# A fused Mamba-2 and pooling block: the first stage's weight subtractions move from GpSimd to VectorE, and the chain from dt gets priority

## The chip, the core and the metric

The kernel runs on one core of a Trainium2 chip. TensorE multiplies, VectorE and ScalarE do elementwise work and move results out of PSUM, GpSimd does a few elementwise operations, and SyncE issues the DMAs. Each engine works its own queue strictly in order and waits on semaphores of the others. The metric is the device time of one execution in microseconds (us), as the median of the runs.

## What is computed

One decoder block over 512 tokens of width 1024, all in float32. The first half, which the change touches:

```python
mod = (silu(c) @ w_ada + b_ada)                       # 6 vectors of 1024: shift, scale, gate, twice
h = rmsnorm(x, norm_mix_w) * (1.0 + scale_m) + shift_m
proj = h @ w_in                                       # z 2048, xbc 3072, dt 32, pool 1024, gates 2048
z, xbc, dt_raw, u_pool, gate_logits = split(proj)
xbc = silu(causal_depthwise_conv(xbc, conv_w, conv_b))
dt = softplus(dt_raw + dt_bias)
a_cont = -exp(a_log)
y = ssd_chunked_scan(x32 * dt, dt * a_cont, bmat, cmat)   # 4 groups of 8 heads, 4 chunks of 128 tokens
# in the scan: a_cs = cumsum(dt * a_cont); decay exp(a_cs[l] - a_cs[s]); states carried over the chunks
```

After it come the skip and the gate by silu(z), a group norm, the branch products, the pooling mixer, the merge, and an MLP with squared ReLU.

## The kernel before

Activations lie transposed: 128 channels on the partitions, 512 tokens along the row. Each float32 product is made of three matmuls in a fast format: a weight block is split into a rounded high half (ScalarE casts it, L131) and the remainder (a subtraction, L132), and so is the activation; high by high, high by low and low by high are summed (`mm3`, L141 to L143). A `unit` is eight blocks of 128 by 128 against h, 24 matmuls into one PSUM bank.

**The first stage (L216 to L283)** is written in the order that the engines keep (`manual_schedule`). ScalarE takes the Silu of c (L225) and TensorE spreads it over the partitions; ScalarE copies that to `cbc` (L235). ScalarE squares the eight tiles of x (L232), VectorE adds the squares as a tree (L230), TensorE sums over the partitions (L164), and `rstd` makes R, the reciprocal norm, spread over partitions in a PSUM bank (L176 to L185). `warm(n)` (L211) issues n small matmuls without a use. Then eight steps, k = 0 to 7, each for 128 channels of h:

- `ada(j)` (L157) forms 128 entries of the vector `mod` on VectorE, from a transfer of 512 KB: a product with `cbc`, summed along the row, and a short read of the accumulator. Each step needs two, the scale and the shift of its channels.
- L250 turns a scale into `amod` = (1 + scale) * norm weight; L265 scales x by it and by R; L266 (ScalarE) adds the shift and rounds to the high half; L271 forms the low half.
- the weights for step k (`wstart`, 896 columns: dt padded to 128, then B, C and four tiles of xs for group 0) are loaded, cast on ScalarE and subtracted on **GpSimd** (`load_unit(..., pool)`, L132), two steps ahead; GpSimd also copies dt's 32 low columns next to the high ones (L268), so that two matmuls do for dt what takes three elsewhere.
- TensorE runs 18 matmuls (L281) into six banks and two for dt (L283) into a seventh.

**Behind it** a scheduler orders the instructions by the order of the code and by priority. ScalarE copies the six banks out (L294). Then **the chain from dt** (L299 to L338): bias (L305), four transposes (L308), softplus as a series on VectorE (L311 to L325, with one exponential, L314, on ScalarE), times -exp(a_log) (L315, L326), cumulative sums by a triangular matmul (L328), `ncs` (L329), transposes back (L332), and the sums and their exponentials to DRAM (L333 to L336), from where they come back spread over partitions (`mt`, L424; L484). `conv` (L344 to L350) makes the convolution and Silu of the six tiles.

**A group of the scan** (`ssd_group`, a generator) goes through its four chunks: mt and its exponentials (L424 to L433), transposes of xs (L437), times dt (`xdt`, L439). It yields, and other units are issued in between. After the yield come the state products: `xd`, the decayed inputs (L451), and their matmul (L454), then the rest of the chunk.

Buffers are slots handed out first in, first out: 50 of 512 columns (`S`), four for raw weights (`RAW`), eight for split weights (`HL`), and eight PSUM banks, three of them (`PU`) for units and five (`PS`) for the rest. The order in which code gives a slot back decides who gets it next.

Of the kernel before, what the change touches and what calls it, by code (L numbers as in the profile page):

```python
# [19 lines left out]
NC = 4  # L20
# [12 lines left out]
NPAR = _n  # L33
# [25 lines left out]
def block_kernel(tc, xT, crow, arow, par, adaT, wstart, wz, wx, wpool_in, wgate, wpw, wbs, wbp, wout, wup, wdn, out):  # L59
    nc = tc.nc  # L60
    act, dve, pool, pe, sp = nc.scalar, nc.vector, nc.gpsimd, nc.tensor, nc.sync

    with (
# [12 lines left out]
        S = slots("s", NSLOT)  # L76
# [9 lines left out]
        par_t = sb.tile([P, NPAR + 0], F32, name="par_t")  # L86
# [129 lines left out]
        with tc.manual_schedule():  # L216
            raw0 = RAW.get()
            crow_t = raw0[:1]
            sp.dma_start(crow_t, crow)
            xs0 = [S.get() for _ in range(8)]  # L220
            for k in range(8):
                sp.dma_start(xs0[k], xT[k])
            sp.dma_start(par_t[:, :NPAR], par)
            warm(6)
            act.activation(crow_t, crow_t, AF.Silu)  # L225
            cps = [PU.get(), PU.get()]
            for i in range(2):
                pe.matmul(cps[i], ones[:1, :], crow_t[:, i * T:(i + 1) * T], start=True, stop=True)
            sq = [S.get() for _ in range(8)]
            add = lambda i, j: dve.tensor_tensor(sq[i], sq[i], sq[j], ALU.add)  # L230
            for k in range(8):
                act.activation(sq[k], xs0[k], AF.Square)  # L232
                if k in (4, 6):
                    i = k // 2 - 2
                    act.copy(cbc[:, i * T:(i + 1) * T], cps[i])  # L235
                for i, j in ((), ((0, 1),), (), ((2, 3), (0, 2)), (), ((4, 5), (0, 4)), ((0, 6),), ((0, 7),))[k]:
                    add(i, j)
            ssum = sq[0]
            S.put(*sq[1:])
            PU.put(*cps)  # L240
            RAW.put(raw0)
            warm(10)
            ps = PU.get()
            column_sums(ps, [ssum], 0, NC)
            S.put(ssum)
            warm(4)
# [6 lines left out]
            scale(0)  # L253
            R = rstd(ps, DM, 0, NC, S)
            PU.put(ps)
            warm(8)
            ada(0, EARLY)
            first = [PS.get() for _ in range(8 - NPU)] + [PU.get() for _ in range(NPU - 1)]
            ws = [load_unit(wstart[i], 896, pool) for i in range(2)]
            for k in range(8):  # L260
                hi, lo = S.get(F32R), S.get(F32R)
                h.append((hi, lo))
                t = S.get()
                shift = mod[:, k:k + 1]
                dve.scalar_tensor_tensor(t, xs0[k], amod[:, k:k + 1], R, ALU.mult, ALU.mult)  # L265
                act.activation(hi, t, AF.Identity, bias=shift)  # L266
                w = ws.pop(0)
                pool.tensor_copy(w[0][0][:, NH:2 * NH], w[0][1][:, :NH].bitcast(F32))  # L268
                if 0 < k < 7:
                    scale(k + 1)  # L270
                dve.scalar_tensor_tensor(lo, t, shift, hi.bitcast(F32), ALU.add, ALU.subtract)  # L271
                S.put(t)
                if k == 0:
                    scale(1)
                if k < 7:
                    ada(k + 1, EARLY)
                if k < 6:
                    ws.append(load_unit(wstart[k + 2], 896, pool))
# [8 lines left out]
        SZ.put(*early[2:])  # L287

        took = [None]
        for u in range(1, 7):  # L290
# [3 lines left out]
            act.copy(took[u], first[u])  # L294
        PU.put(*first[8 - NPU:])
        PS.put(*first[1:8 - NPU])


        r_ = slice(0, NH)  # L299
        w_ = NC * NH  # L300
        v, cs_t, ecs_t = S.get(), S.get(), S.get()
        tmp = [S.get() for _ in range(4)]
        sp.dma_start(ea, arow[0:1, :].broadcast_to([P, NH]))
        e, s, s2, q = (t[:, :w_] for t in tmp)
        act.activation(v[:2 * NH], first[0][:2 * NH], AF.Identity, bias=col("dtb", rows=2 * NH))  # L305
        tk = PU.get()
        for c in range(NC):
            pe.transpose(tk[:, 2 * c * NH:2 * (c + 1) * NH], v[:2 * NH, c * P:(c + 1) * P], ident[:2 * NH, :2 * NH])  # L308
        dtf, ncf = dtk.rearrange("p c h -> p (c h)"), ncs.rearrange("p c h -> p (c h)")
        both = tk[:, :2 * w_].rearrange("p (c a h) -> p c a h", c=NC, a=2)  # L310
        dve.tensor_copy(dtk, both[:, :, 0, :])  # L311
        dve.tensor_tensor(dtk, dtk, both[:, :, 1, :], ALU.add)
        dve.scalar_tensor_tensor(e, dtf, -1.0, dtf, ALU.mult, ALU.max)
        act.activation(e, e, AF.Exp, scale=-1.0)  # L314
        act.activation(ea, ea, AF.Exp)  # L315
        dve.tensor_scalar(s, e, 2.0, None, ALU.add)
        dve.reciprocal(s, s)
        dve.tensor_tensor(s, s, e, ALU.mult)
        dve.tensor_tensor(s2, s, s, ALU.mult)
        dve.tensor_scalar(q, s2, 1.0 / 15, None, ALU.mult)  # L320
        for d in (13, 11, 9, 7, 5, 3):
            dve.scalar_tensor_tensor(q, q, 1.0 / d, s2, ALU.add, ALU.mult)
        dve.scalar_tensor_tensor(q, q, 1.0, s, ALU.add, ALU.mult)
        dve.tensor_scalar(dtf, dtf, 0.0, None, ALU.max)
        dve.scalar_tensor_tensor(dtf, q, 2.0, dtf, ALU.mult, ALU.add)  # L325
        dve.tensor_tensor(  # L326
            q.rearrange("p (c h) -> p c h", c=NC), dtk, ea.unsqueeze(1).broadcast_to([P, NC, NH]), ALU.mult)
        pe.matmul(tk[:, :w_], tri, q, start=True, stop=True)  # L328
        dve.tensor_copy(ncf, tk[:, :w_])  # L329
        tk2 = first[0]  # L330
        for c in range(NC):
            pe.transpose(tk2[r_, c * P:(c + 1) * P], ncs[:, c, :], ident)  # L332
        act.activation(cs_t[r_], tk2[r_], AF.Copy, scale=-1.0)  # L333
        act.activation(ecs_t[r_], tk2[r_], AF.Exp, scale=-1.0)
        sp.dma_start(cs_d, cs_t[r_])
        sp.dma_start(ecs_d, ecs_t[r_])  # L336
        PU.put(tk)
        S.put(v, cs_t, ecs_t, *tmp)  # L338


        def conv(ps, j, o=None):
# [61 lines left out]
        def ssd_group(g):  # L403
# [17 lines left out]
            for c in range(NC):  # L421
# [14 lines left out]
                for i in range(4):  # L436
# [2 lines left out]
                dve.tensor_tensor(  # L439
                    v3(xdt), v3(ps), dtk[:, c, heads].unsqueeze(2).broadcast_to([P, HG, 64]), ALU.mult)  # L440
                PS.put(ps)
                yield
                yo = None
                if c > 0:
# [2 lines left out]
                        pe.matmul(yo[:, i * P:(i + 1) * P], prev[:, i * P:(i + 1) * P], cT[:, cc],  # L447
                                  start=True, stop=True)
                if c < 3:
                    xd = S.get()  # L450
                    dve.tensor_tensor(  # L451
                        v3(xd), v3(xdt), decg[:, c, :].unsqueeze(2).broadcast_to([P, HG, 64]), ALU.mult)
# [12 lines left out]
                    prev = nprev  # L465
# [367 lines left out]
```

## Time and profile before

| | us |
|---|---|
| median of 3 runs (lowest, highest) | 998.27 (997.61, 998.98) |
| the profiled execution | 997.95 |
| its span, first to last instruction | 996.2 |
| TensorE busy in the span | 973.7 (98%) |
| VectorE busy | 623.8 (63%) |
| ScalarE busy | 482.3 (48%) |
| GpSimd busy | 84.7 (9%) |

Times in the profile count from the start of the span. The busy time of TensorE is modelled from pipelined matmuls: a matmul of 512 columns shows a duration of some 390 ns, and the next one starts 0.23 us after it began. So the distance of two starts, not the duration, is what a matmul costs in a full stretch. In an idle time the releaser named is the one that came last.

### The profile page before, as it was taken

Reading aid. Unit: us, or ns where it says so; the run is one execution under the profiler, and the core shown is the slowest. Engines: PE = TensorE matmul, PEld = TensorE weight load, DVE = VectorE, ACT = ScalarE, POOL = GpSimd, SP = SyncE. Lnnn points to the kernel's source line nnn. Section 1 sums busy time; section 2 is a strip of 40 time slices with the busy share of each in tenths; the row PEclk is TensorE's granted clock in tenths of the full one; section 3 lists DMA queues with packets and bytes.
Section 4 is the critical chain, followed back from the end, with each engine's and each line's share of the span. In section 5 each row is a group of like instructions: output and inputs, shape, how many; then the busy total and the mean of one; then the engine's idle time right before and its main releaser. Section 6 shows DMA issues by size and latency. Waiting matters only on the chain.

```text
span 996.2 us, 12196 instructions
## 1 busy us (share of the span) xinstructions
PE 973.7 (98%) x4732; PEld 802.8 (81%) x4732; DVE 623.8 (63%) x887; ACT 482.3 (48%) x718; POOL 84.7 (9%) x79
## 2 busy tenths in 40 slices
PE   7899999999999999999999999999999999999996
PEld 6678777888778878788888888988888888888886
DVE  5978877586777776979775565654344334434443
ACT  5277999579648932553422343443133223313342
POOL 3510210211012012210000000000000000000000
PEclk8999999999999999999999999999999999999998
DMA  9725542442354233436886444032323232232302
GB/s 355 278 92 172 152 124 91 125 136 88 90 134 125 88 114 95 127 106 220 279 272 200 137 167 162 1 111 101 101 89 106 85 106 89 102 106 85 106 1 85
DMA packets 58620, 129.55 MB, mean 130 GB/s; under 512 B 4609, under 2 KB 29313, under 8 KB 58562
## 3 DMA queue, kind: packets, MB, share of 16 engines
q1 hardware_dynamic: 58562, 128.77, 40.1%
q8 instruction: 37, 0.61, 0.3%
q14 instruction: 21, 0.17, 0.1%
HBM read 126.53 MB, written 2.23 MB: 129 GB/s over the span
## 4 chain that ended last, share of the span: by engine, by line
PE 79%; ACT 8%; DVE 7%; DMA 2%; issue 2%; POOL 1%; SPq 1%; DVEq 0%; ACTq 0%; POOLq 0%
PE ps L141 25%; PE ps L142 24%; PE ps L143 24%; DMA mt<-cs_d 2%; ACT hl L131 1%; ACT L433 1%; DVE sz L157 1%; DVE xs L157 1%; PE ps L470 1%; PE ps L454 1%; ACT L350 1%; PE ps L447 1%; PE ps L281 1%; ACT L378 1%; DVE s L271 1%
## 5 line engine op out<-in xcount | busy, mean ns | idle before, releaser
L141 PE MATMUL ps<-s,hl 128*128 128x512 f32 (+1 forms) x1272 | 490.9, 386 | 1.3 <-ACT pad L529 1.2
L142 PE MATMUL ps<-s,hl 128*128 128x512 f32 (+1 forms) x1272 | 486.4, 382 | 0.0
L143 PE MATMUL ps<-s,hl 128*128 128x512 f32 (+1 forms) x1272 | 486.4, 383 | 0.0
L131 ACT CAST hl<-raw 128x1024 fp32r<-128x1024 f32 (+1 forms) x161 | 167.4, 1042 | 276.4 <-PE ps L142 269.0
L141 PEld LDWEIGHTS ps<-s,hl 128*128 128x128 f32 x1272 | 239.3, 188 | 50.4 <-issue 3.5
L142 PEld LDWEIGHTS ps<-s,hl 128*128 128x128 f32 x1272 | 239.4, 188 | 46.8 <-issue 1.4
L143 PEld LDWEIGHTS ps<-s,hl 128*128 128x128 f32 x1272 | 239.3, 188 | 46.8 <-issue 1.0
L132 DVE TENSOR_TENSOR hl<-raw,hl 128x1024 fp32r<-128x1024 f32 x153 | 189.9, 1243 | 126.5 <-ACT hl L131 123.5
L663 DVE SCALAR_TENSOR_TENSOR xs<-ps,mod,xs 128x512 f32<-128x512 f32 (+1 forms) x46 | 31.3, 680 | 106.8 <-PE ps L143 106.7
L111 ACT CAST s<-sz 128x512 fp32r<-128x512 f32 x52 | 31.5, 620 | 52.9 <-DVE sz L709 42.3
L157 DVE CUSTOM_DVE_ANT_0 raw<-raw,cbc,par_t 128x1024 f32<-128x1024 f32 x32 | 40.9, 1279 | 19.1 <-DMA raw<-adaT 19.0
L112 DVE TENSOR_TENSOR s<-sz,s 128x512 fp32r<-128x512 f32 x52 | 35.0, 689 | 22.8 <-ACT s L111 22.7
L433 ACT ACTIVATE mt<-mt,ncs 128x128 f32<-128x128 f32 x128 | 41.7, 392 | 13.2 <-POOL mt L429 12.9
L346 DVE SCALAR_TENSOR_TENSOR s<-ps,par_t,s 128x511 f32<-128x511 f32 (+2 forms) x54 | 40.2, 744 | 7.4 <-ACT s L344 6.9
L281 PE MATMUL ps<-s,hl 128*128 128x512 f32 x144 | 36.7, 410 | 5.8 <-ACT s L266 5.8
L281 PEld LDWEIGHTS ps<-s,hl 128*128 128x128 f32 x144 | 27.5, 196 | 14.3 <-ACT s L266 7.9
L429 POOL TENSOR_SCALAR_AFFINE_SELECT mt<-mt 128x1024 f32<-128x1024 f32 x16 | 19.5, 1224 | 215.4 <-ACT cd L426 99.0
L350 ACT ACT_TABLE_LOAD x19 | 24.4, 1283 | 7.0 <-DVE s L346 6.7
L433 ACT ACT_TABLE_LOAD x20 | 25.7, 1283 | 0.3
L492 ACT ACTIVATE s<-sz 128x512 f32<-128x512 f32 x16 | 10.1, 628 | 26.6 <-DVE sz L491 26.6
L111 ACT CAST s<-s 128x512 fp32r<-128x512 f32 x16 | 9.9, 622 | 25.5 <-DVE s L542 25.3
L709 DVE TENSOR_TENSOR sz<-sz 128x512 f32<-128x512 f32 x32 | 21.7, 684 | 0.0
(164 smaller groups left out, 783.7 us busy)
## 6 DMA issues: line engine op xcount, KB each, us to landing
raw<-adaT SPq DMA_DIRECT2D x32, 512.0 KB, 4.2
raw<-wup SPq DMA_DIRECT2D x32, 512.0 KB, 3.3
raw<-wdn SPq DMA_DIRECT2D x32, 512.0 KB, 3.3
raw<-wx SPq DMA_DIRECT2D x18, 512.0 KB, 3.5
raw<-wz SPq DMA_DIRECT2D x16, 512.0 KB, 4.0
mt<-cs_d SPq DMA_DIRECT2D x16, 512.0 KB, 5.9
raw<-wbs SPq DMA_DIRECT2D x16, 512.0 KB, 3.3
raw<-wgate SPq DMA_DIRECT2D x16, 512.0 KB, 3.7
```

Source lines behind the costliest of these rows:

```text
L111: act.copy(hi, src)
L112: dve.tensor_tensor(lo, src, hi.bitcast(F32), ALU.subtract)
L131: act.copy(hi[:, :w], r[:, a:a + w])
L132: (low or dve).tensor_tensor(lo[:, :w], r[:, a:a + w], hi[:, :w].bitcast(F32), ALU.subtract)
L141: pe.matmul(ps, whi, xhi[:, t0:t1], start=start, stop=False)
L142: pe.matmul(ps, whi, xlo[:, t0:t1], start=False, stop=False)
L143: pe.matmul(ps, wlo, xhi[:, t0:t1], start=False, stop=stop)
L157: dve.tensor_tensor_reduce(r, r, cbc, 1.0, col("b_ada", j), ALU.mult, ALU.add, mod[:, j:j + 1])
L281: pe.matmul(first[u], w[u][i // 2], h[k][i % 2], start=k == 0 and i == 0, stop=k == 7 and i == 2)
L346: dve.scalar_tensor_tensor(t[:, sh:], ps[:, :T - sh], w(3 - sh), t[:, sh:], ALU.mult, ALU.add)
L350: act.activation(o, t, AF.Silu)
L433: act.activation(m[:, i, :], m[:, i, :], AF.Exp, bias=ncs[:, c, g * HG + i:g * HG + i + 1])
```

## The change

In the first stage, GpSimd no longer subtracts. `begin(k)` loads and casts the weights of step k at the step's start, `end` subtracts on VectorE between the scaling and the low half, and GpSimd keeps its copy of 32 columns. `amod` is formed on ScalarE. The squares are added one after another into one buffer; half of `cbc` is copied by VectorE; fewer warming matmuls are issued. In the last step dt's two matmuls stand ahead of the last six. The whole chain from dt stands under `high_priority` and ahead of the copies of the six banks, so its bank `tk` is given back before two banks of the first stage are. In a chunk, `xd` is formed ahead of the yield.

```diff
@@ first stage
-            add = lambda i, j: dve.tensor_tensor(sq[i], sq[i], sq[j], ALU.add)
             for k in range(8):
                 act.activation(sq[k], xs0[k], AF.Square)
-                if k in (4, 6):
-                    i = k // 2 - 2
-                    act.copy(cbc[:, i * T:(i + 1) * T], cps[i])
-                for i, j in ((), ((0, 1),), (), ((2, 3), (0, 2)), (), ((4, 5), (0, 4)), ((0, 6),), ((0, 7),))[k]:
-                    add(i, j)
+                if k == 1:
+                    act.copy(cbc[:, :T], cps[0])
+                if k == 4:
+                    dve.tensor_copy(cbc[:, T:], cps[1])
+                if k:
+                    dve.tensor_tensor(sq[0], sq[0], sq[k], ALU.add)
...
             def scale(k):
-                ada(8 + k, EARLY)
-                dve.tensor_scalar(amod[:, k:k + 1], mod[:, 8 + k:9 + k], 1.0, col("nmix", k), ALU.add, ALU.mult)
+                act.activation(amod[:, k:k + 1], mod[:, 8 + k:9 + k], AF.Identity,
+                               bias=col("nmix", k), scale=col("nmix", k))
+            def begin(k):
+                r, hi, lo = RAW.get(), HL.get(F32R), HL.get(F32R)
+                sp.dma_start(r[:, :896], wstart[k])
+                act.copy(hi[:, :896], r[:, :896])
+                return r, hi, lo
+            def end(r, hi, lo):
+                dve.tensor_tensor(lo[:, :896], r[:, :896], hi[:, :896].bitcast(F32), ALU.subtract)
+                pool.tensor_copy(hi[:, NH:2 * NH], lo[:, :NH].bitcast(F32))
...
-            ws = [load_unit(wstart[i], 896, pool) for i in range(2)]
             for k in range(8):
...
+                w = begin(k)
+                if k:
+                    ada(8 + k, EARLY)
+                    scale(k)
+                    ada(k, EARLY)
                 dve.scalar_tensor_tensor(t, xs0[k], amod[:, k:k + 1], R, ALU.mult, ALU.mult)
                 act.activation(hi, t, AF.Identity, bias=shift)
-                w = ws.pop(0)
-                pool.tensor_copy(w[0][0][:, NH:2 * NH], w[0][1][:, :NH].bitcast(F32))
-                if 0 < k < 7:
-                    scale(k + 1)
+                w = end(*w)
                 dve.scalar_tensor_tensor(lo, t, shift, hi.bitcast(F32), ALU.add, ALU.subtract)
...
                 for i in range(3):
+                    if k == 7 and i == 2:
+                        dt_unit()
                     for u in range(1, 7):
                         pe.matmul(first[u], w[u][i // 2], h[k][i % 2], start=k == 0 and i == 0, stop=k == 7 and i == 2)
-                for i in range(2):
-                    pe.matmul(first[0], w[0][0], h[k][i], start=k == 0 and i == 0, stop=k == 7 and i == 1)
+                if k < 7:
+                    dt_unit()
@@ the chain from dt, its lines unchanged
+        with tc.high_priority():
+            ...
+        PU.put(tk)
         for u in (6, 5, 1, 2, 3, 4):
             act.copy(took[u], first[u])
@@ ssd_group, after xdt (the same three lines are taken out behind the yield)
+                if c < 3:
+                    xd = S.get()
+                    dve.tensor_tensor(
+                        v3(xd), v3(xdt), decg[:, c, :].unsqueeze(2).broadcast_to([P, HG, 64]), ALU.mult)
                 yield
```

What the scheduler makes of it, at three places. On VectorE, one step of the first stage before, from the scaling of one step to that of the next (L157 is `ada`, its second row the read of the sum; L250 forms `amod`, L271 the low half):

```order
L265 SCALAR_TENSOR_TENSOR s_75_373<-s_14_105,amod,ps_34_187 128x512
L157 ISA xs_6_94,mod<-xs_6_94,cbc,par_t 128x1024
L157 ISA mod 128x1
L250 TENSOR_SCALAR amod<-mod,par_t 128x1
L271 SCALAR_TENSOR_TENSOR s_74_372<-s_75_373,mod,s_73_371 128x512
L157 ISA xs_6_94,mod<-xs_6_94,cbc,par_t 128x1024
L157 ISA mod 128x1
L265 SCALAR_TENSOR_TENSOR s_81_411<-s_15_106,amod,ps_34_187 128x512
```

The same step in the changed kernel, where L282 is the scaling, L258 the subtraction of the weights and L285 the low half:

```order
L282 SCALAR_TENSOR_TENSOR s_69_344<-s_14_105,amod,ps_34_179 128x512
L258 TENSOR_TENSOR hl_72_347<-raw_70_345,hl_71_346 128x896
L285 SCALAR_TENSOR_TENSOR s_68_343<-s_69_344,mod,s_67_342 128x512
L157 ISA xs_6_94,mod<-xs_6_94,cbc,par_t 128x1024
L157 ISA mod 128x1
L157 ISA xs_6_94,mod<-xs_6_94,cbc,par_t 128x1024
L157 ISA mod 128x1
```

L250 has left VectorE, L258 has come, and the low half follows the scaling directly behind it.

On ScalarE, the start of the changed kernel (L321 is the exponential of a_log, L225 the Silu of c, L231 the squares):

```order
L321 ACT_TABLE_LOAD
L321 ACTIVATE ea<-ea 128x32
L225 ACT_TABLE_LOAD
L225 ACTIVATE raw_9_99<-raw_9_99 1x1024
L231 ACTIVATE s_21_130<-s_10_101 128x512
L231 ACTIVATE s_22_131<-s_11_102 128x512
```

The first two rows stood near the end of the stage before, at L315, and the list began with L225; on SyncE the transfer of a_log (L309, before L303) now stands first of all.

On TensorE, after two units behind the first stage and group 0's products of B and C, before (L437 transposes a tile of xs; ps_146 is a unit for group 1); the second transpose comes fifteen matmuls behind the first:

```order
L141 MATMUL ps_146_798<-s_49_219,hl_144_794 128x512
L142 MATMUL ps_146_798<-s_50_220,hl_144_794 128x512
L437 MATMUL ps_136_761<-ident,xs_109_577 128x128
L143 MATMUL ps_146_798<-s_49_219,hl_145_795 128x512
L141 MATMUL ps_146_798<-s_55_257,hl_144_794 128x512
L142 MATMUL ps_146_798<-s_56_258,hl_144_794 128x512
```

In the changed kernel the same place (L452 transposes a tile of xs, L334 is the triangular matmul of the chain, ps_156 a unit for group 1):

```order
L141 MATMUL ps_156_850<-s_43_195,hl_154_846 128x512
L142 MATMUL ps_156_850<-s_44_196,hl_154_846 128x512
L143 MATMUL ps_156_850<-s_43_195,hl_155_847 128x512
L452 MATMUL ps_136_749<-ident,xs_109_565 128x128
L141 MATMUL ps_156_850<-s_49_228,hl_154_846 128x512
L142 MATMUL ps_156_850<-s_50_229,hl_154_846 128x512
L143 MATMUL ps_156_850<-s_49_228,hl_155_847 128x512
L141 MATMUL ps_156_850<-s_55_266,hl_154_846 128x512
L142 MATMUL ps_156_850<-s_56_267,hl_154_846 128x512
L143 MATMUL ps_156_850<-s_55_266,hl_155_847 128x512
L334 MATMUL ps_98_504<-s_97_501,tri 128x128
L452 MATMUL ps_150_835<-ident,xs_109_565 128x128
```

The second transpose now stands six matmuls and L334 behind the first, where fifteen matmuls stood; from the end of group 0 on, TensorE's order is that of before.

## Rows read from the trace of the kernel before

**Rows 1.** Table by stretch: length, busy PE, PEld, DVE, ACT, POOL (instructions), clock, DMA share, GB/s

```profile
17.90:65.50 47.60, 41.75 (x176) 32.19 (x175) 44.48 (x54) 16.79 (x23) 25.59 (x16) 0.96 0.67 243
65.50:200.00 134.50, 132.65 (x678) 105.57 (x679) 100.31 (x156) 112.44 (x194) 20.70 (x21) 1.00 0.44 126
200.00:900.00 700.00, 697.57 (x3359) 578.37 (x3358) 429.13 (x600) 306.17 (x430) 36.01 (x35) 1.00 0.39 126
```

**Rows 2.** Timeline, one first-stage step: start, us, engine, line, operation, output<-input [idle<-releaser]

```profile
31.17 0.73 DVE L265 SCALAR_TENSOR_TENSOR s<-s,amod,ps 128x512 f32<-128x512 f32 x1
...
31.94 0.72 ACT L266 ACTIVATE s<-s,mod 128x512 fp32r<-128x512 f32 x1 [4.26 <-DVE s L265]
...
33.15 0.21 DVE L250 TENSOR_SCALAR amod<-mod,par_t 128x1 f32<-128x1 f32 x1
...
33.28 0.74 DVE L271 SCALAR_TENSOR_TENSOR s<-s,mod,s 128x512 fp32r<-128x512 f32 x1
33.57 2.42 POOL L132 TENSOR_TENSOR hl<-raw,hl 128x896 fp32r<-128x896 f32 x1 [2.27 <-ACT hl L131]
33.94 3.15 DVE L157 CUSTOM_DVE_ANT_0 sz<-sz,cbc,par_t 128x1024 f32<-128x1024 f32 x1
35.94 1.21 POOL L268 CAST hl<-hl 128x32 fp32r<-128x32 f32 x1
...
37.01 0.74 DVE L265 SCALAR_TENSOR_TENSOR s<-s,amod,ps 128x512 f32<-128x512 f32 x1
```

**Rows 3.** Timeline, end of the first stage

```profile
57.31 1.28 DVE L157 CUSTOM_DVE_ANT_0 sz<-sz,cbc,par_t 128x1024 f32<-128x1024 f32 x1
...
60.78 4.24 PE L281 MATMUL ps<-s,hl 128*128 128x512 f32 x18
60.99 2.43 DVE L132 TENSOR_TENSOR hl<-raw,hl 128x1024 fp32r<-128x1024 f32 x2
...
64.86 0.62 PE L283 MATMUL ps<-s,hl 128*128 128x512 f32 x2
...
65.54 0.50 PE L141 MATMUL ps<-s,hl 128*128 128x512 f32 x1
```

**Rows 4.** Timeline, start of the kernel

```profile
0.80 1.28 ACT L225 ACT_TABLE_LOAD   x1 [0.80 <-PEq L825]
...
2.29 1.06 ACT L225 ACTIVATE raw<-raw 1x1024 f32<-1x1024 f32 x1 [0.21 <-DMA raw<-crow]
3.88 1.33 ACT L232 ACTIVATE s<-s 128x512 f32<-128x512 f32 x2 [0.54 <-DMA s<-xT]
...
6.29 1.99 ACT L232 ACTIVATE s<-s 128x512 f32<-128x512 f32 x3 [1.07 <-DMA s<-xT]
...
9.31 3.02 DVE L230 TENSOR_TENSOR s<-s,s 128x512 f32<-128x512 f32 x4 [0.25 <-ACT s L232]
...
12.38 1.86 PE L164 MATMUL ps<-ones,s 128*128 128x1 f32 x8 [3.74 <-DVE s L230]
...
17.91 0.75 DVE L265 SCALAR_TENSOR_TENSOR s<-s,amod,ps 128x512 f32<-128x512 f32 x1 [1.36 <-PE ps L185]
```

**Rows 5.** Transfers issued in the first 66 us: count, KB, median us to landing

```profile
ea<-arow SPq DMA_DIRECT2D x1, 16.0 KB, 4.4
```

**Rows 6.** Timeline, ScalarE, after the first stage

```profile
78.69 0.63 ACT L350 ACTIVATE xs<-s 128x512 f32<-128x512 f32 x1
...
82.29 0.63 ACT L350 ACTIVATE xs<-s 128x512 f32<-128x512 f32 x1 [2.50 <-DVE s L346]
```

**Rows 7.** Timeline, TensorE, after the first stage

```profile
79.43 0.27 PE L437 MATMUL ps<-ident,xs 128*128 128x128 f32 x1
```

**Rows 8.** Waits of TensorE in the whole run: us in total, times, longest

```profile
PE ps L454 <- DVE s L451: 2.3, 4, 0.8
```

**Rows 9.** Table by stretch, a pause of TensorE and what followed, columns as in rows 1

```profile
24.70:26.90 2.20, 0.02 (x2) 0.00 (x1) 2.20 (x4) 0.78 (x2) 0.79 (x1) 1.00 1.02 402
28.40:31.50 3.10, 3.10 (x9) 2.45 (x9) 3.10 (x3) 0.00 (x0) 2.91 (x2) 0.51 1.03 412
```

More of the change, by code (lines that the diff above doesn't have):

```diff
@@ L222, in block_kernel @@
                 sp.dma_start(xs0[k], xT[k])
-            sp.dma_start(par_t[:, :NPAR], par)
+            sp.dma_start(par_t, par)
             warm(6)
@@ L248, in scale @@
+            S.put(*sq)
+            warm(3)
             def scale(k):
-                ada(8 + k, EARLY)
-                dve.tensor_scalar(amod[:, k:k + 1], mod[:, 8 + k:9 + k], 1.0, col("nmix", k), ALU.add, ALU.mult)
+                act.activation(amod[:, k:k + 1], mod[:, 8 + k:9 + k], AF.Identity,
[5 more added lines that the diff above has]
+                return r, hi, lo
@@ L252, in block_kernel @@
+            def end(r, hi, lo):
+                dve.tensor_tensor(lo[:, :896], r[:, :896], hi[:, :896].bitcast(F32), ALU.subtract)
+                pool.tensor_copy(hi[:, NH:2 * NH], lo[:, :NH].bitcast(F32))
+                RAW.put(r)
+                HL.put(hi, lo)
+                return [(hi[:, o:o + P], lo[:, o:o + P]) for o in range(0, 896, P)]
             h = []
-            scale(0)
+            ada(8, EARLY)
             R = rstd(ps, DM, 0, NC, S)
             PU.put(ps)
-            warm(8)
@@ L257, in block_kernel @@
             ada(0, EARLY)
+            scale(0)
+            warm(3)
             first = [PS.get() for _ in range(8 - NPU)] + [PU.get() for _ in range(NPU - 1)]
-            ws = [load_unit(wstart[i], 896, pool) for i in range(2)]
             for k in range(8):
@@ L264, in block_kernel, with dt_unit @@
                 shift = mod[:, k:k + 1]
+                w = begin(k)
[3 more added lines that the diff above has]
+                    ada(k, EARLY)
                 dve.scalar_tensor_tensor(t, xs0[k], amod[:, k:k + 1], R, ALU.mult, ALU.mult)
                 act.activation(hi, t, AF.Identity, bias=shift)
-                w = ws.pop(0)
-                pool.tensor_copy(w[0][0][:, NH:2 * NH], w[0][1][:, :NH].bitcast(F32))
-                if 0 < k < 7:
-                    scale(k + 1)
+                w = end(*w)
                 dve.scalar_tensor_tensor(lo, t, shift, hi.bitcast(F32), ALU.add, ALU.subtract)
                 S.put(t)
[L273 to L278, printed above, removed]
+                def dt_unit():
+                    for i in range(2):
+                        pe.matmul(first[0], w[0][0], h[k][i], start=k == 0 and i == 0, stop=k == 7 and i == 1)
                 for i in range(3):
+                    if k == 7 and i == 2:
+                        dt_unit()
                     for u in range(1, 7):
                         pe.matmul(first[u], w[u][i // 2], h[k][i % 2], start=k == 0 and i == 0, stop=k == 7 and i == 2)
-                for i in range(2):
-                    pe.matmul(first[0], w[0][0], h[k][i], start=k == 0 and i == 0, stop=k == 7 and i == 1)
+                if k < 7:
+                    dt_unit()
         PU.put(R)
@@ L287, in block_kernel @@
         SZ.put(*early[2:])
+        with tc.high_priority():
+            r_ = slice(0, NH)
+            w_ = NC * NH
+            v, cs_t, ecs_t = S.get(), S.get(), S.get()
+            tmp = [S.get() for _ in range(4)]
+            sp.dma_start(ea, arow[0:1, :].broadcast_to([P, NH]))
+            e, s, s2, q = (t[:, :w_] for t in tmp)
+            act.activation(v[:2 * NH], first[0][:2 * NH], AF.Identity, bias=col("dtb", rows=2 * NH))
+            tk = PU.get()
+            for c in range(NC):
+                pe.transpose(tk[:, 2 * c * NH:2 * (c + 1) * NH], v[:2 * NH, c * P:(c + 1) * P], ident[:2 * NH, :2 * NH])
+            dtf, ncf = dtk.rearrange("p c h -> p (c h)"), ncs.rearrange("p c h -> p (c h)")
+            both = tk[:, :2 * w_].rearrange("p (c a h) -> p c a h", c=NC, a=2)
+            dve.tensor_copy(dtk, both[:, :, 0, :])
+            dve.tensor_tensor(dtk, dtk, both[:, :, 1, :], ALU.add)
+            dve.scalar_tensor_tensor(e, dtf, -1.0, dtf, ALU.mult, ALU.max)
+            act.activation(e, e, AF.Exp, scale=-1.0)
+            act.activation(ea, ea, AF.Exp)
+            dve.tensor_scalar(s, e, 2.0, None, ALU.add)
+            dve.reciprocal(s, s)
+            dve.tensor_tensor(s, s, e, ALU.mult)
+            dve.tensor_tensor(s2, s, s, ALU.mult)
+            dve.tensor_scalar(q, s2, 1.0 / 15, None, ALU.mult)
+            for d in (13, 11, 9, 7, 5, 3):
+                dve.scalar_tensor_tensor(q, q, 1.0 / d, s2, ALU.add, ALU.mult)
+            dve.scalar_tensor_tensor(q, q, 1.0, s, ALU.add, ALU.mult)
+            dve.tensor_scalar(dtf, dtf, 0.0, None, ALU.max)
+            dve.scalar_tensor_tensor(dtf, q, 2.0, dtf, ALU.mult, ALU.add)
+            dve.tensor_tensor(
+                q.rearrange("p (c h) -> p c h", c=NC), dtk, ea.unsqueeze(1).broadcast_to([P, NC, NH]), ALU.mult)
+            pe.matmul(tk[:, :w_], tri, q, start=True, stop=True)
+            dve.tensor_copy(ncf, tk[:, :w_])
+            tk2 = first[0]
+            for c in range(NC):
+                pe.transpose(tk2[r_, c * P:(c + 1) * P], ncs[:, c, :], ident)
+            act.activation(cs_t[r_], tk2[r_], AF.Copy, scale=-1.0)
+            act.activation(ecs_t[r_], tk2[r_], AF.Exp, scale=-1.0)
+            sp.dma_start(cs_d, cs_t[r_])
+            sp.dma_start(ecs_d, ecs_t[r_])
+        PU.put(tk)
+        S.put(v, cs_t, ecs_t, *tmp)
         took = [None]
@@ L296, in block_kernel @@
         PS.put(*first[1:8 - NPU])
[L299 to L338, printed above, removed]
         def conv(ps, j, o=None):
```

14 lines of the change are left out of this document (4 added, 10 removed).

## Prediction

> **What bounds the kernel now.** I read the table by stretch first, then timelines of the stretch that is not full. From 65.5 us to 900 us TensorE is busy for 830.2 of 834.5 us at full clock, and no change of order can give back more there than the 4.3 us that are left [rows 1]. The first stage, 17.9 to 65.5 us, is different: TensorE is busy for 41.8 of 47.6 us, VectorE for 44.5 [rows 1]. The timeline of one step says why. A step lasts from one L265 to the next, 31.17 to 37.01, or 5.84 us, and VectorE is never free in it [rows 2]. TensorE's work for a step is twenty matmuls: 18 of them start between 60.78 and 64.86, 0.227 us each, so twenty take 4.55 us [rows 3]. VectorE sets the pace of this stage, by 1.3 us a step, and within the step one instruction is odd: the second L157 lasts 3.15 us [rows 2], while the same operation at 57.31, with GpSimd idle, lasts 1.28 us [rows 3]. GpSimd's subtraction runs from 33.57 to 35.99, and the slow L157 ends 1.1 us behind it [rows 2]: the two did not run at the same time.
>
> **The change, part by part.** All times are of the profiled execution, which took 997.95 us (span 996.2); the median of the runs is 998.27, and I carry differences over to the median.
>
> *The step.* VectorE now runs, per step: two L157 at their undisturbed 1.28 us (2.5 us with the overlap of neighbours), the scaling (0.66 us from start to start of its twin L271, 33.28 to 33.94 [rows 2]), the subtraction, and the low half (0.66). The subtraction on VectorE has no row at 896 columns. At 1024 columns two take 2.43 us, 1.2 each [rows 3]; seven eighths of that is 1.05. L250 (0.21 us) moves to ScalarE, where the next L157 covers it: the scaling needs it only 1.2 us later. The sum is 2.5 + 0.66 + 1.05 + 0.66 = 4.87; I take 4.85. Below it lies TensorE's own 4.55. The high half that TensorE waits for is ready 0.85 us behind the scaling (31.94 to 32.66, after a scaling that began at 31.17 and ended at 31.90, with some 0.1 to hand over [rows 2]). The low half follows 1.7 us behind the scaling, and TensorE needs it after six matmuls, 1.4 us after the high half: no wait.
>
> *The start.* ScalarE now does the exponential of a_log before everything else. That is one more table load, 1.28 us [rows 4], and a small activation, ahead of the Silu at 2.29, and its transfer goes to the head of SyncE's queue, past c and x, each of which is issued one issue later; with the load in front of the Silu it would begin near 4.0. ScalarE waited 0.54 and 1.07 us for x in its squares [rows 4], so most of the 1.7 us is absorbed and the last square ends about when it did. But VectorE's additions are now one chain on one buffer, with a copy among them: from the third square (about 8.05) six additions at 0.755 (four took 3.02 [rows 4]) and a copy of some 0.65 end at 13.2, where the row has 12.33. All that follows (L164 at 12.38, the first scaling at 17.91 [rows 4]) slips by 0.9. The bounds: 0 if the chain keeps up, and +3 if the row of a_log, which landed 4.4 us after its issue in a full queue [rows 5], takes as long in an empty one; the row of c, in an empty queue, cost ScalarE only 0.21 us [rows 4], and that is the nearer case. The Trainium skill, "ScalarE: Activation LUTs", section "What ACT_TABLE_LOAD costs", says that a switch of table costs 1.28 us and a drain of about 1.38 more. Here the activation behind the load waits 0.21 us, for its data [rows 4], so the trace does not show the drain; by the page the start would be 1.4 us later, and the time 993.6 us.
>
> *The stage.* The first scaling at 18.8; first step 0.66 + 1.05 + 0.66 to 21.2; six more steps of 4.85 to 50.3; two L157 and the scaling of the last step to 53.5; high half 54.3; twenty matmuls to 58.8. Before, the last of them ends at 65.48 (64.86 + 0.62 [rows 3]). **The stage gains 6.7 us.** The weight buffers are now released by VectorE at the step's own time and not two steps ahead, so the transfers of the next units leave later, yet the third still leaves a step before the end and its subtraction is behind the stage's own.
>
> *The chain from dt.* It is not on the path: TensorE was full over it. What counts is what TensorE meets in its order. Before, fifteen matmuls stand between the first two transposes of xs (L437); now only six and the chain's triangular matmul (the order in the section on the change). The first was asked for at 79.43 [rows 7], when its input had been ready for 0.1 us (78.69 + 0.63); the second input was ready at 82.92 [rows 6], that is 17.4 us behind the end of the stage (65.5). VectorE's list up to there is the same convolution and the same chain, so I keep 17.4. With the four transposes of dt now inside the stage, that is 59.2 + 17.4 = 76.6; TensorE asks at 59.2 + 13.9 − 0.4 + 0.2 + 1.9 = 74.8 (the same 13.9 us, less the dt transposes, one matmul more, then transpose, six matmuls and L334). **It waits 1.8 us.** Bounds: 0, if the chain's earlier start on VectorE (its copies no longer wait for six on ScalarE) carries the convolution with it, and 3, if the first transpose comes too early as well. Behind the instruction stands all of TensorE's queue. The unit that takes the chain's bank is queued behind it too, after ncs, which is out by then.
>
> *The decayed inputs.* TensorE waited four times, 2.3 us, for L451 [rows 8]. It is now issued a step earlier; two of the four lie where the order is otherwise unchanged. I take half, **1.2 us**, with 0 and 2.3 as bounds. It adds no instruction, and holds one buffer longer.
>
> The sum: −6.7 + 1.8 − 1.2 = −6.1, or **992.2 us** on the median.
>
> **The rivals.**
> 1. *The waits do not come* (bound 0 above). Then 990.4. For it: the order was made to fit readiness before, to 0.1 us. Against: ScalarE now has four copies and a table load ahead of the chain's exponential.
> 2. *GpSimd's small copy starves.* It stays on GpSimd after each subtraction, and the dt matmul needs it. In the row it waited for the L157 and took 1.21 [rows 2]; in the last step four VectorE instructions with two inputs follow without a gap (L285, three L132), 0.7 + 3 × 1.15 = 4.1 us. If it waits for all of them, the dt matmuls stand 1.5 us, and with a start that slips by a further 1.5 the time is 995.2. The Trainium skill, "SBUF — State Buffer", section "Who interferes with whom", says that a VectorE operation with two SBUF inputs and a GpSimd operation that reads SBUF exclude each other for a whole instruction, whoever starts first. That is a rule against what stays on GpSimd; rows 2 agree with it, both ways round. For: VectorE has no gap any more. Against: the copy of the row got in as soon as one instruction ended.
> 3. *Nothing measurable.* A late start (3 us for 0.9) and waits of 3 leave a gain of 2.8, and a spell of TensorE's low clock, as from 28.4 to 31.5, where it was granted 0.51 (the 1.2 GHz level) after it had stood idle from 24.7 to 26.9 [rows 9], would take 1.5 more if it came after the stage: 997.0. In the stage TensorE's spare 0.3 us a step would repay it.
> 4. *Slower: L157 stays slow.* If the 3.15 us are not GpSimd's doing, but another access to the same buffers, the step becomes 4.85 + 1.87 = 6.7, seven steps cost 6.1 more than before, and with the start (0.9) and the waits (1.8) less 1.2 the time is 1005.9. It decides from an excess of 0.87 us a step: there the stage's gain of 6.1 is gone. Against: the undisturbed row in the same stage.
>
> **How the numbers follow.** Forecast (the sum within its bounds, 991 to 994.5) 0.48; rival 1, 0.18; rival 2, 0.15; rival 3, 0.11; rival 4, 0.08. This kernel's measurement tells 0.2%, 2 us, from no change. Faster: the first three, 0.81; same: 0.11; slower: 0.08. The range from 989.5 (rival 1 with all of the 2.3 us) to 996.8 leaves out rival 4 and most of rival 3, and little at the lower end.
>
> **What would show it.** L157 at 1.28 us throughout the stage; a step of 4.85 us; L164 near 13.3; the stage's last matmul near 58.8; TensorE idle some 2 us ahead of the second transpose of xs, and no longer ahead of the state matmul L470 (L454 before). A step above 5.5 us, or over 5 us of new idle time on TensorE between 60 and 160 us, would make the prediction wrong.

## The result, and the profile after

The changed kernel takes **993.05 us** (median of 4 runs, 992.86 to 993.42), the kernel before 998.62 us beside it (4 runs, 997.61 to 999.56): a ratio of 0.9935, 95% interval 0.9917 to 0.9954. By the medians it is 5.6 us faster (the interval allows 4.6 to 8.3), in the range that was given and 0.9 us above the forecast of 992.2. The profiled execution took 992.94 us (span 991.2) against 997.95 (996.2).

The table by stretch, cut at the same landmarks as [rows 1] (first scaling, first unit behind the stage); columns as there:

```profile
20.90:61.53 40.63, 39.35 (x171) 30.20 (x170) 39.95 (x59) 19.56 (x30) 4.87 (x8) 1.00 0.73 256
61.53:200.00 138.47, 136.39 (x706) 108.72 (x707) 102.63 (x159) 112.81 (x195) 22.40 (x21) 1.00 0.44 129
200.00:900.00 700.00, 698.58 (x3352) 579.47 (x3351) 426.88 (x595) 305.20 (x431) 35.73 (x35) 1.00 0.39 126
```

The stage lasts 40.6 us where it lasted 47.6 [rows 1, 3, 4], TensorE idles 1.3 us in it instead of 5.9, and GpSimd works 4.9 us instead of 25.6. VectorE is still busy for nearly all of it. One step of the stage in the changed kernel, on VectorE and GpSimd, in the timeline (start, length, engine, line; the answer to [rows 2]):

```profile
25.64 0.74 DVE L282 SCALAR_TENSOR_TENSOR s<-s,amod,ps 128x512 f32<-128x512 f32 x1
26.30 1.08 DVE L258 TENSOR_TENSOR hl<-raw,hl 128x896 fp32r<-128x896 f32 x1
...
27.30 0.74 DVE L285 SCALAR_TENSOR_TENSOR s<-s,mod,s 128x512 fp32r<-128x512 f32 x1
...
27.52 0.60 POOL L259 CAST hl<-hl 128x32 fp32r<-128x32 f32 x1 [4.14 <-DVE hl L258]
...
27.97 1.27 DVE L157 CUSTOM_DVE_ANT_0 sz<-sz,cbc,par_t 128x1024 f32<-128x1024 f32 x1
...
29.17 1.28 DVE L157 CUSTOM_DVE_ANT_0 sz<-sz,cbc,par_t 128x1024 f32<-128x1024 f32 x1
...
30.38 0.74 DVE L282 SCALAR_TENSOR_TENSOR s<-s,amod,ps 128x512 f32<-128x512 f32 x1
```

Both L157 last 1.28 us, and a step lasts 4.74 us (25.64 to 30.38) where it lasted 5.84 [rows 2]. GpSimd's small copy ends with the one VectorE instruction beside it (L285) and keeps nobody. But the stage begins late. The start of the changed kernel (the answers to [rows 4]):

```profile
4.56 0.23 ACT L321 ACTIVATE ea<-ea 128x32 f32<-128x32 f32 x1 [2.48 <-DMA ea<-arow]
4.81 1.28 ACT L225 ACT_TABLE_LOAD   x1
6.11 1.05 ACT L225 ACTIVATE raw<-raw 1x1024 f32<-1x1024 f32 x1
...
9.70 3.23 ACT L231 ACTIVATE s<-s 128x512 f32<-128x512 f32 x6
...
10.37 1.49 DVE L237 TENSOR_TENSOR s<-s,s 128x512 f32<-128x512 f32 x2 [1.44 <-ACT s L231]
...
12.37 3.07 DVE L237 TENSOR_TENSOR s<-s,s 128x512 f32<-128x512 f32 x4
...
15.49 1.86 PE L164 MATMUL ps<-ones,s 128*128 128x1 f32 x8 [2.60 <-DVE s L237]
...
20.90 0.75 DVE L282 SCALAR_TENSOR_TENSOR s<-s,amod,ps 128x512 f32<-128x512 f32 x1 [1.24 <-PE ps L185]
```

The last square of the kernel before, which [rows 4] leaves out:

```profile
10.17 0.64 ACT L232 ACTIVATE s<-s 128x512 f32<-128x512 f32 x1
```

ScalarE stands 2.48 us for a_log's row, with a second table load and the Silu of c queued behind it (6.11 where it was 2.29). The last square ends at 12.93 where it ended at 10.81, the additions at 15.44 where they ended at 12.33, and the first scaling is at 20.90 where it was 17.91. Behind the stage, the waits of TensorE (releaser, us in total, times, longest), without two in the tail:

```profile
PE ps L141 <- ACT pad L545: 1.2, 1, 1.2
PE ps L486 <- DVE mt L449: 1.2, 1, 1.2
...
PE ps L142 <- DVE s L112: 0.6, 1, 0.6
...
PE ps L141 <- ACT s L351: 0.4, 1, 0.4
PE ps L470 <- DVE s L459: 0.2, 1, 0.2
PE ps L141 <- ACT sz L393: 0.2, 1, 0.2
```

The state matmul's wait for the decayed inputs has gone from 2.3 us [rows 8] to 0.2 (L470 on L459). New are 1.2 us of L486 on the decay matrix and 0.6 of L142.

Three landmarks of the timelines split each profiled execution: the first scaling; the first unit's matmul behind the stage; and the first sum L170 (four matmuls) of the tail. All experiments are read by them:

| kernel | first scaling | unit behind the stage | L170 | stage | behind it |
|---|---|---|---|---|---|
| before | 17.91 | 65.54 | 976.60 | 47.63 | 911.06 |
| after | 20.90 | 61.53 | 971.07 | 40.63 | 909.54 |
| after, once more | 20.83 | 61.42 | 970.94 | 40.59 | 909.52 |

The start costs 3.0 us, the stage gives 7.0 (7.4, if the four transposes of dt, 0.4 us, which now lie in it, are set aside), what lies behind gives 1.5 (1.1 without them), and the rest of the tail was 0.5 us longer in this execution: 3.0 − 7.0 − 1.5 + 0.5 = −5.0. The second execution agrees within 0.04 us in the stage and 0.02 us behind it, so these two lengths are sharper than the time of a run. The kernel before was profiled once. The first scaling is not as steady: it came at 16.56 to 18.23 us in the three profiled kernels with the start of before, and at 20.34 to 20.90 in the three profiles with a_log first.

### The profile page after: what moved, and what is told of

Read it like the earlier page. It is cut to its first block, busy times and chain, and to the rows that moved or that the text cites. A ratio compares the mean times of both kernels' runs of the same rounds, so it can differ in the third digit from the quotient of the medians.

```text
span 991.2 us, 12146 instructions
## 1 busy us (share of the span) xinstructions
PE 972.0 (98%) x4708; PEld 800.1 (81%) x4708; DVE 617.8 (62%) x888; ACT 482.9 (49%) x724; POOL 63.9 (6%) x71
## 4 chain that ended last, share of the span: by engine, by line
PE 83%; ACT 7%; DVE 4%; DMA 3%; issue 2%; POOL 0%; SPq 0%; DVEq 0%; POOLq 0%; ACTq 0%
PE ps L141 25%; PE ps L142 25%; PE ps L143 25%; PE ps L295 3%; DMA mt<-cs_d 2%; PE ps L486 1%; ACT hl L131 1%; PE ps L470 1%; PE ps L466 1%; ACT L448 1%; DVE s L361 1%; DVE hl L132 1%; ACT L393 1%; ACT mt L448 1%; PE ps L185 0%
## 5 line engine op out<-in xcount | busy, mean ns | idle before, releaser
L142 PE MATMUL ps<-s,hl 128*128 128x512 f32 (+1 forms) x1272 | 485.4, 382 | 0.6 <-DVE s L112 0.6
L131 ACT CAST hl<-raw 128x1024 fp32r<-128x1024 f32 x153 | 160.1, 1048 | 273.9 <-PE ps L142 268.8
L142 PEld LDWEIGHTS ps<-s,hl 128*128 128x128 f32 x1272 | 239.3, 188 | 48.0 <-DVE s L112 1.9
L157 DVE CUSTOM_DVE_ANT_0 raw<-raw,cbc,par_t 128x1024 f32<-128x1024 f32 x32 | 40.9, 1279 | 18.4 <-DMA raw<-adaT 18.2
L449 DVE TENSOR_TENSOR mt<-mt,ps 128x1024 f32<-128x1024 f32 x16 | 19.4, 1214 | 5.3 <-ACT mt L448 2.9
```

What stands on the lines that cost most here:

```text
L131: act.copy(hi[:, :w], r[:, a:a + w])
L142: pe.matmul(ps, whi, xlo[:, t0:t1], start=False, stop=False)
```

## The experiments

**GpSimd's subtraction alone.** In the kernel before, VectorE subtracts, still two steps ahead:

```diff
-            ws = [load_unit(wstart[i], 896, pool) for i in range(2)]
+            ws = [load_unit(wstart[i], 896, dve) for i in range(2)]
...
-                    ws.append(load_unit(wstart[k + 2], 896, pool))
+                    ws.append(load_unit(wstart[k + 2], 896, dve))
```

> The kernel before, with one edit: the subtractions of the first stage's weights are on VectorE, still two steps ahead; GpSimd keeps its copy of 32 columns, all else stays. Theory A: L157 lasts 3.15 us because GpSimd's subtraction reads and writes beside it. Then every L157 lasts 1.28 us, a step falls from 5.84 to about 5.05 us (two times 1.28, 0.66, 0.21, 1.05, 0.66, less overlaps), six steps of eight gain, and the time is 993 to 995. Theory B: L157 is slow by another access to the same buffers. Then it stays at 3.15 us, the step grows to about 6.9 us, and the time is 1003 to 1005.

It took 994.59 us, 0.9948 of the kernel before [0.9933, 0.9963]. The timeline of one step:

```profile
29.07 0.74 DVE L265 SCALAR_TENSOR_TENSOR s<-s,amod,ps 128x512 f32<-128x512 f32 x1
...
29.22 0.21 POOL L268 CAST hl<-hl 128x32 fp32r<-128x32 f32 x1 [4.77 <-DVE hl L132]
...
29.73 1.28 DVE L157 CUSTOM_DVE_ANT_0 sz<-sz,cbc,par_t 128x1024 f32<-128x1024 f32 x1
...
31.84 1.28 DVE L157 CUSTOM_DVE_ANT_0 sz<-sz,cbc,par_t 128x1024 f32<-128x1024 f32 x1
...
33.05 1.09 DVE L132 TENSOR_TENSOR hl<-raw,hl 128x896 fp32r<-128x896 f32 x1
34.05 0.74 DVE L265 SCALAR_TENSOR_TENSOR s<-s,amod,ps 128x512 f32<-128x512 f32 x1
```

Every L157 lasts 1.28 us and the step 4.98. The stage is 42.74 us long (18.23 to 60.97), 4.9 shorter than before, and the stretch behind it 911.29, as before. Theory A holds: this one edit brings 4.9 of the stage's 7.0 us. The other 2.1 are the rest of the change in the stage, read from the rows and not tested part by part: six steps of 4.98 us become 4.74 (L250 has left VectorE), the first step of 5.86 us becomes 4.74 too, and 0.5 goes back at the end.

**Reading or writing?** In the kernel before, GpSimd fills with zeros instead of subtracting, so the low half of these weights is left out of the products:

```diff
-                    (low or dve).tensor_tensor(lo[:, :w], r[:, a:a + w], hi[:, :w].bitcast(F32), ALU.subtract)
+                    if low is None:
+                        dve.tensor_tensor(lo[:, :w], r[:, a:a + w], hi[:, :w].bitcast(F32), ALU.subtract)
+                    else:
+                        pool.memset(lo[:, :w].bitcast(F32), 0.0)
```

> The kernel before, with GpSimd's subtraction replaced by a fill of the same 896 columns with zeros on GpSimd: the low half of the first stage's weights is left out of the products, their matmuls stay. GpSimd then writes as much as before but reads nothing there. Theory A: what shuts out L157 is GpSimd's reading. Then L157 lasts 1.28 us throughout, also beside the fill, the step falls to TensorE's 4.55 us, and the time is 991 to 993. Theory B: GpSimd's writing shuts it out as well. Then L157 beside the fill is longer by the overlap, 2 us or more, and the time lies between 993 and 998.

It took 990.55 us in one run, just below the 991 to 993 expected, with a first scaling at 16.56 us; the argument rests on the rows and not on this time. The timeline; lines stand three further down here, so L160 is `ada`, L135 the fill, L271 the small copy, L268 the scaling:

```profile
31.95 0.85 POOL L135 MEMSET hl<- 128x896 f32 x1 [2.43 <-PE ps L284]
32.16 1.28 DVE L160 CUSTOM_DVE_ANT_0 xs<-xs,cbc,par_t 128x1024 f32<-128x1024 f32 x1
32.74 0.76 POOL L271 CAST hl<-hl 128x32 fp32r<-128x32 f32 x1
33.36 0.08 DVE L160 DVE_READ_ACCUMULATOR2_ANT mod<- 128x1 f32 x1
33.36 0.75 DVE L268 SCALAR_TENSOR_TENSOR s<-s,amod,ps 128x512 f32<-128x512 f32 x1
```

The fill runs while L160 runs, and neither is longer for it: through the stage every fill lasts 0.84 or 0.85 us and every L160 1.27 or 1.28. The copy behind the fill reads, and it ends only behind L160. So it is GpSimd's reading that the long VectorE operation excludes, as theory A said; writing beside it cost nothing here. VectorE's step falls to 3.98 us, and TensorE is then the bound (36.9 of 37.0 us busy between 20 and 57 us).

**a_log late.** The changed kernel with a_log out of the way of the Silu:

```diff
+                if k == 2:
+                    sp.dma_start(ea, arow[0:1, :].broadcast_to([P, NH]))
+                if k == 6:
+                    act.activation(ea, ea, AF.Exp)
...
-            sp.dma_start(ea, arow[0:1, :].broadcast_to([P, NH]))
-            act.activation(ea, ea, AF.Exp)
```

> The changed kernel, with the transfer of a_log issued in the third step of the first stage and its exponential taken in the seventh, so that neither stands ahead of the Silu of c. Theory A: the first scaling is 3.0 us later than before the change (20.90 against 17.91) because ScalarE waits 2.48 us at its head for a_log's transfer. Then the first scaling comes back to 18 to 19, and the time falls by 2 to 3 us, from 993.05 to 990 or 991. Theory B: the slip comes from the additions in one chain and the copy of cbc on VectorE, or from x and c arriving late in any case. Then the first scaling stays at 20 to 21 and the time at 993. Theory C: the start is won, but the stage then waits for the transfers of its weights, which have the same rate; then steps grow above 4.74 us and less than 1 us is left.

> The run with a_log late once more, as the base of the two beside it on the same chip: 990.9 us, ratio to the kernel before 0.991.

It took 990.92 us (0.9913 [0.9896, 0.9930]), and 991.45 the second time (0.9921 [0.9909, 0.9934]). The additions, TensorE's column sum and the first scaling in the first profile:

```profile
7.23 1.49 DVE L237 TENSOR_TENSOR s<-s,s 128x512 f32<-128x512 f32 x2 [1.11 <-ACT s L231]
...
9.24 3.07 DVE L237 TENSOR_TENSOR s<-s,s 128x512 f32<-128x512 f32 x4
...
12.36 1.87 PE L164 MATMUL ps<-ones,s 128*128 128x1 f32 x8 [2.60 <-DVE s L237]
...
17.77 0.75 DVE L282 SCALAR_TENSOR_TENSOR s<-s,amod,ps 128x512 f32<-128x512 f32 x1 [1.24 <-PE ps L185]
```

The column sum and the scaling stand where they stood before the change [rows 4], with the additions in one chain and the copy on VectorE. From the third square on, the chain and the copy last 5.1 us in both kernels (7.23 to 12.31 here, 10.37 to 15.44 in the changed kernel); they end 3.1 us earlier because the square is ready 3.1 us earlier, and then they end when the tree did (12.33). So theory A holds: the late start is due to a_log's place ahead of the Silu, its transfer and the second table load together, and the chain of additions costs nothing once the squares come in time. Whether the tree would have been quicker behind the late squares was not tested. In the six profiles with a_log late the first scaling comes at 17.18 to 18.87 us.

Yet of 3.1 us only some 2 arrive. The stage is 41.27 us, 0.64 longer, and the stretch behind it 910.50, 0.96 longer:

```profile
50.26 1.99 ACT L131 CAST hl<-raw 128x1024 fp32r<-128x1024 f32 x2
52.15 0.72 ACT L283 ACTIVATE s<-s,mod 128x512 fp32r<-128x512 f32 x1
...
89.99 1.09 PE L488 MATMUL ps<-mt,s 128*64 128x128 f32 x16 [2.27 <-DVE mt L451]
```

In the stage's last step two casts for the next units stand in front of the rounding L283, which starts 0.48 us after the scaling has ended (52.15) and not 0.04 (54.84 in the changed kernel). Behind the stage L488 now waits 2.27 us for the decay matrix.

In the second profile, which was the slowest of its six runs, that stretch took 912.14. Table by stretch of this execution, the wait and what followed:

```profile
88.70:91.10 2.40, 0.14 (x1) 0.02 (x1) 1.68 (x2) 2.40 (x7) 0.00 (x0) 1.00 1.06 230
...
92.00:94.00 2.00, 2.00 (x9) 1.53 (x6) 1.87 (x6) 1.97 (x4) 0.00 (x0) 0.62 0.76 181
94.00:96.00 2.00, 2.00 (x6) 1.51 (x6) 0.95 (x3) 1.99 (x5) 0.14 (x1) 0.53 0.96 328
```

After the same wait TensorE was granted 0.62 and 0.53 (near its 1.2 GHz level) for some 4 us; in the first profile it was granted 1.00 there too. That is the other 1.6 us. With a first scaling that came 1.1 us later (18.87 against 17.77) it makes the 2.7 us between the two profiled executions (993.65 and 990.91); what spread the other runs, no profile shows.

**The wait on the decay matrix.** In group 0, chunk 1's small operations are queued behind chunk 0's exponentials and product:

```diff
+                    behind = g == 0 and c == 1
+                    with tc.issue_after(last_exp) if behind else nullcontext():
                         act.activation(cdg[:, c, :], m[:, :, P - 1], AF.Exp)
+                    with tc.issue_after(last_mul) if behind else nullcontext():
                         dve.tensor_tensor(decg[:, c, :], m[:, :, P - 1], ncs[:, c, heads], ALU.add)
```

> The run with a_log late, with one more edit: in group 0 the three small operations of chunk 1 (two exponentials, one addition, L443 to L445) are queued behind chunk 0's eight exponentials and its product, on ScalarE and VectorE. In the run with a_log late, ScalarE had chunk 0's matrix ready at 84.13 us, but stood 2.62 us for chunk 1's transfer, and TensorE waited 2.3 us on L488 for the product. Theory A: that order is the wait's cause. Then the eight exponentials start at about 84.2, the product ends at about 88.0 in place of 89.84, TensorE's wait on L488 falls to about 0.5 us, and the time falls by 1.5 to 1.9 us, from 990.9 to about 989.2. Theory B: the wait only moves to the next chunk or to the decayed inputs. Then the time stays within 0.5 us of 990.9.

It took 991.00 us (990.00 to 992.25; 0.9918 [0.9904, 0.9931]): theory B, as far as the time tells. The waits of TensorE show both halves:

```profile
PE ps L494 <- DVE mt L456: 0.6, 1, 0.6
...
PE ps L142 <- DVE s L112: 0.3, 1, 0.3
PE ps L478 <- DVE s L467: 0.3, 1, 0.3
PE ps L494 <- DVE dec L447: 0.3, 1, 0.3
```

The cause was right: the exponentials start at 83.79, and the 2.27 us have become 0.3. But three others, of 0.60, 0.34 and 0.33 us, stand further on (at 115.0, 156.2 and 342.8 us) where the run with a_log late had none, and the stretch is 909.96 us, only 0.5 shorter. When TensorE comes 2 us earlier, the next operand is late in its turn.

**The chain's place.** On the run with a_log late, the chain from dt goes back behind the copies, without priority:

```diff
-        with tc.high_priority():
+        took = [None]
+        ...
+        for u in (6, 5, 1, 2, 3, 4):
+            act.copy(took[u], first[u])
+        ...
+        if True:
             r_ = slice(0, NH)
```

> The run with a_log late, with the chain from dt taken out of high priority and put back behind the six bank copies, as it stood before the change. The stage is untouched, so its first scaling (17.77 us) and its end stay. Theory A: priority and place bring the sums out earlier, and TensorE's wait for the decay matrix would grow without them. Then cs_d leaves a few us behind 74.2, TensorE waits more than 2.3 us on L488, and the time is 992 to 994. Theory B: TensorE's order is made to fit whatever the chain's place, so the place is worth nothing. Then the idle time behind the stage stays within 0.7 us of what it was, and the time within 0.7 us of 990.9. Theory C: the place costs something, because with it both of ScalarE's first two chunks' small exponentials meet the same wait; then the time falls below 990.

> The changed kernel once more, beside the two others on the same chip, as their base: 993.05 us as before, within 0.5 us. Every theory expects the same of it.

> The run with a_log late and the chain from dt back behind the copies, without priority, once more beside its base on one chip. Theory A: the place of the chain costs 1.8 us in the changed order, as the single comparison gave it: then 989.1 against 990.9 in this call too, and the order of the two holds round by round. Theory B: the difference was that of two chips and two starts: then the two agree within 0.7 us.

It took 989.13 us (988.71 to 989.64; 0.9898 [0.9884, 0.9912]) beside the changed kernel's 992.26 (991.55 to 993.08; 0.9929 [0.9917, 0.9942]; 0.8 below the 993.05 expected), and once more 989.71 (989.27 to 989.97) beside the 991.45 of the run with a_log late (990.59 to 993.65): lower by 1.7 us, with no run of one among the other's; between the fastest runs of the two it is 1.3. It is the fastest kernel of this study. The place of the chain, one of the change's three parts, costs time in this order; place and priority went back together, and which of the two it is was not tested. The stretch behind the stage is 909.12 and 909.08 us, against 910.50 with priority. Theory A is out. Theory C's result came, but its reason didn't: ScalarE meets the same wait without priority. TensorE's timeline (second profile) shows another:

```profile
91.06 1.12 PE L472 MATMUL ps<-s,s 128*128 128x512 f32 x2 [1.54 <-DVE s L461]
...
97.26 1.09 PE L488 MATMUL ps<-mt,s 128*64 128x128 f32 x16
```

L488 stands at 97.26 instead of 89.99, with more unit work ahead of it, and doesn't wait. With priority the chain's sums leave earlier (the transfer of cs_d is issued at 74.20 us, without it at 76.85 in the second profile, with the first scaling at 17.77 in both), and L488 stands seven us earlier; but the matrix comes by a transfer of 512 KB that is issued at 76.51 and used from 82.73 on, and chunk 1's from 85.77 on. The order was early, the transfers were not; that this is the cause is read from these times, not tested by a run of its own. The state matmul L472 waits instead, 1.5 us. TensorE's idle time explains 0.8 of the 1.4 us between the two stretches (3.1 against 3.9); where the other 0.6 lies was not settled.

**That wait, too.** In the kernel just told of, chunk 1's addition is queued behind chunk 0's decayed inputs on VectorE:

```diff
+                    with tc.issue_after(xd0) if g == 0 and c == 1 else nullcontext():
                         dve.tensor_tensor(decg[:, c, :], m[:, :, P - 1], ncs[:, c, heads], ALU.add)
```

> As the one beside it (a_log late, chain without priority), with chunk 1's addition L444 in group 0 queued behind chunk 0's decayed inputs on VectorE. There VectorE stood 2.48 us for chunk 1's transfer with chunk 0's decayed inputs behind it, and TensorE waited 1.72 us on L472. Theory A: the wait goes: 987.4 us, 1.7 less than the run beside it. Theory B: most of it comes back in the chunks behind, as 1.6 of 2.3 us did with chunk 0's matrix: then about 988.6 us, a difference too small to be told.

989.95 us (989.80 to 991.05; 0.9907 [0.9894, 0.9921]), by the time the same as 989.71 beside it; the stretch is 909.54, 0.4 longer. Theory B, and a little worse: VectorE now waits for ScalarE's cast of weights in front of the same operation, and 1.1 of 1.7 us remain on the state matmul (its longest wait).

**The decayed inputs.** The changed kernel with `xd` back behind the yield:

```diff
-                if c < 3:
-                    xd = S.get()
-                    dve.tensor_tensor(v3(xd), v3(xdt), ...)
                 yield
...
+                    xd = S.get()
+                    dve.tensor_tensor(v3(xd), v3(xdt), ...)
```

> The changed kernel, with the decayed inputs (L459) back behind the yield. Theory A: forming them early saves the waits of TensorE on them, 2.3 us before the change and 0.2 after. Then the time rises by 1 to 2 us, to 994 or 995, and TensorE's waits on that line come to about 2 us. Theory B: other waits take their place either way (L486 waited 1.19 us for L449 in the changed kernel). Then those go when xd goes back, and the time stays within 0.5 us of 993.05.

993.91 us (993.46 to 994.23; 0.9940 [0.9925, 0.9955]): the time alone can't tell this from 993.05, but the stretch behind the stage can. It is 910.63 us, 1.1 longer than the changed kernel's, and TensorE's wait is back:

```profile
PE ps L469 <- DVE s L466: 1.5, 2, 1.0
...
PE ps L485 <- DVE mt L449: 1.0, 1, 1.0
```

Theory A: early decayed inputs are worth 1.1 us. L485's wait doesn't go when they go back.

## Why the prediction held, step by step

- **What bounds the stage.** Right. The 3.15 us of the second L157 were GpSimd's reading beside it, shown twice: it goes with the subtraction, and stays away with a fill. The Trainium skill, "SBUF — State Buffer", section "Who interferes with whom", says that a VectorE instruction with two SBUF inputs contends with a GpSimd instruction that reads SBUF and not with one that only writes it. The fill agrees (0.85 us beside an L160 of 1.28), and so does the small copy: 0.21 us beside the scaling, which takes one input from PSUM, and 0.60 beside L285, which takes both from SBUF. Rival 4 (L157 stays slow) is out.
- **The step.** 4.85 forecast, 4.74 measured. From the first scaling to the last matmul the sum had 40.0 us; it is 40.2 (20.90 to 61.08), the dt transposes' 0.4 included.
- **The start** was mis-sized, and is a step that failed: 0.9 us forecast, 3.0 measured, the upper bound. The working had the late Silu absorbed, so that the last square ends about when it did, and put the 0.9 on the chain of additions. The last square ended 2.1 us later (12.93 against 10.81), and the additions ended 1.0 us further behind it than before (2.5 against 1.5); with a_log late the two stand at 10.60 and 12.31, as before the change. The row of c (a wait of 0.21 us) was not the nearer case: a_log's row, 16 KB in 128 rows of 128 bytes, landed 3.7 us after its issue in an empty queue, not far from the 4.4 of [rows 5]. The Trainium skill, "ScalarE: Activation LUTs", section "What ACT_TABLE_LOAD costs", adds a drain of 1.38 us to the load. The trace does not agree: the activation behind the load at 4.81 starts at 6.11, 1.30 us later, data in hand.
- **The second transpose of xs** did not wait, and is the other step that failed: 1.8 us forecast, none measured. The 1.8 us were read off the order wrongly: the first L452 writes ps_136, the second ps_150. It transposes the same tile for the next chunk, and that tile was ready:

```profile
76.53 0.38 PE L334 MATMUL ps<-s,tri 128*128 128x128 f32 x2
76.75 0.27 PE L452 MATMUL ps<-ident,xs 128*128 128x128 f32 x1
76.78 0.47 PE L141 MATMUL ps<-s,hl 128*128 128x512 f32 x1
```

  On this point rival 1 was right. In its place TensorE waits 1.2 us on the decay matrix, which no term had. With the chain back behind the copies (and a_log late) TensorE has no such wait, so the chain's place brought it.
- **The decayed inputs**: 1.2 us forecast, 1.1 measured with them put back.
- **GpSimd's copy** (rival 2) holds up nobody: 0.60 us, no wait of TensorE on it. TensorE's low clock behind a pause (in rival 3) did not come in the changed kernel between 22 and 980 us, where it was granted 1.00; it came once in the run with a_log late.

So the mechanism of the stage was right, but that the forecast of 992.2 is as near 993.05 as it is was luck, because two errors offset each other: the start was 2.1 us worse, and the stretch behind the stage 1.7 better (−1.1, where +1.8 − 1.2 was forecast).

## What to carry to other kernels

A two-input VectorE operation that is odd in length beside a GpSimd operation is best tested by replacing GpSimd's work with a fill: if the length goes back, GpSimd's reads belong elsewhere. A small transfer set at the head of a queue is not early for the engine that must wait for it in order; put its consumer where that engine has a gap. And work that a scheduler pulls ahead because a chain got priority is early only if the transfers in that chain keep up: here the kernel with a_log late was 1.3 to 1.7 us faster with the chain behind the copies and without priority.

## What was unexpected of the hardware

After a pause of 2.27 us TensorE's granted clock stayed at 1.00 in one execution and fell to 0.62 and 0.53 in another of the same kernel, at a cost of 1.6 us. After pauses of 1.5 and 1.7 us (L472, chain without priority) it stayed at 1.00. And a transfer of 16 KB that nothing stood before took 3.7 us to land.
